# Issuing the stores of whole row tiles from ScalarE's DMA queue instead of SyncE's

## The chip, the core and the metric

The kernel runs on one core of a Trainium2 chip. A core has five engines, each with its own instruction stream: TensorE (PE in the profile, with PEld for its weight loads), VectorE (DVE), ScalarE (ACT), GpSimd (POOL) and SyncE (SP), which computes nothing and here only issues DMAs. An engine works through its stream strictly in order; where an instruction waits for a semaphore, all behind it wait too. DMAs are carried out by 16 DMA engines, and are issued by an instruction on SyncE or ScalarE, each of which has a queue of its own. The metric is the device time of one execution in microseconds, the median of several runs.

## What is computed

```python
batch, seq, dim = 8, 1024, 768          # x: float32 (8, 1024, 768)
# w_qkv: float32 (768, 2304)
rms = np.sqrt(np.mean(x ** 2, axis=-1, keepdims=True) + eps)
x_norm = x / rms * gamma
return np.matmul(x_norm, w_qkv)         # float32 (8, 1024, 2304)
```

So each of the 8192 rows of x is normalised, and the result is multiplied by one weight matrix.

## The kernel before

The rows are cut into 64 row tiles of 128 rows, and two neighbouring row tiles make a pair. The columns of the result are cut into three chunks of 768. One pair and one chunk make a 2 x 2 block problem (two row tiles, two halves of 384 columns, two halves of the 768 summed elements), and the kernel computes it with seven block products instead of eight: sums of blocks of x and sums of blocks of the weights are multiplied, and the results are put together from the products and held intermediate results. Such a product is three matmuls of 128x384.

The work on one pair passes through these steps:

- `load_x` (L417): SyncE issues the load of a row tile, 384 KB, into one of ten buffers.
- `pstat` and `prms` (L616, L620): ScalarE sums the squares and takes the root, `precip` (L625): VectorE takes the reciprocal.
- `pcast` (L630): VectorE scales the tile and casts it to float16, two instructions for a pair.
- `pxbar` (L634): SyncE issues a DMA transpose of the tile, so that the summed elements lie on the partitions.
- `osum` (L648): GpSimd makes four sums of blocks from the two transposed tiles, once both have landed, in one of three buffers.
- `product` (L668): TensorE, seven for each of the three chunks, into PSUM banks called a, b and c. A later product is added into the same bank after an earlier one has been copied out.
- `hold` (L677 on ScalarE, L675 on VectorE) copies an intermediate result out of PSUM; `join` (L684, VectorE) and `last` (L688, ScalarE) write finished blocks of 128x384 into the row tile's output buffer.
- `rstore` (L520): one DMA stores a whole row tile of 128x2304 float32, 1152 KB. In the very last pair `pstore` (L712) and `end_out` (L707) store pieces instead.

The order of instructions on each engine is written out by hand. The plan is a list of (time, operation) entries that is sorted by time and then issued; its times only order the instructions and make nothing happen at a moment. The first 15 pairs are listed in `PLAN`. From the 16th pair (`STEADY = 15`) on, a loop gives each chunk seven slots of 0.4875 us and each pair 21 slots, so 10.24 us, with the operations at fixed slots. A tile framework then adds the semaphores that the data need. It also gives each DMA one of eight DMA semaphores in turn, and a DMA is not issued before the one that had the same semaphore, eight DMAs earlier, has landed.

In the loop, a pair's first row tile is stored at slot 8.0 and its second at slot 15.6 of the last chunk, in the stream of SyncE, between the loads and the transposes of later pairs. In SyncE's stream the sequence of one pair is: store, store, load, load, transpose, transpose.

Of the kernel before, what the change touches and what calls it, by code (L numbers as in the profile page):

```python
# [350 lines left out]
def kernel(  # L351
# [8 lines left out]
    nc = tc.nc  # L360
# [10 lines left out]
    of = out.flatten_outer_dims()  # L371
# [3 lines left out]
    P = 128  # L375
# [37 lines left out]
    X, XB, XT, RS, OUT, WF, PM, PT = {}, {}, {}, {}, {}, {}, {}, {}  # L413
# [102 lines left out]
        else:  # L516
            nc.scalar.activation(out=o, in_=pm, func=AF.Copy, scale=RS[t], bias=0.0)

    def rstore(t):
        nc.sync.dma_start(out=of[t * P:(t + 1) * P, :], in_=OUT[t])  # L520
        if t in lent:
            spare.append(lent.pop(t))

# [2 lines left out]
    def at(time, fn, *args):  # L526
        plan.append((time, len(plan), fn, args))
# [181 lines left out]
    def pstore(p, c, i, *half):  # L709
# [4 lines left out]
    N_CH = N // (2 * CW)  # L714
    ops = {"load_x": load_x, "load_w": load_w, "conv": conv, "cast": cast, "stat": stat, "recip": recip, "tr": tr, "cp": cp, "mm": mm,
           "idle": idle, "gamma_in": gamma_in, "evac": evac, "rstore": rstore, "tr_half": tr_half, "cp_half": cp_half,
           "bound": bound, "fold": fold, "bound_tr": bound_tr, "bound_top": bound_top, "bound_all": bound_all,
           "scales": scales, "quad": quad, "tsum": tsum, "pstat": pstat, "prms": prms, "precip": precip, "pcast": pcast,
# [4 lines left out]
    for p in range(STEADY, MT // 2):  # L723
        for c in range(N_CH):
            z = HEAD_END + 7 * SLOT * ((p - STEADY) * N_CH + c)

            def when(u, fn, *args):
                at(z + u * SLOT, fn, *args)

            if c == 0:  # L730
                for i in range(2):
                    t = 2 * p + i
                    when(-96.3 + 0.1 * i, load_x, t)
                    when(-64 + 7 * i, pstat, t)
                    when(-48.1 + 1.3 * i, pcast, t)
                    when(-33.1 + 0.1 * i, pxbar, t)
                when(-54.5, prms, p)
                when(-48.3, precip, p)
                for i, q in enumerate(SUMS):
                    when(-15 + 0.01 * i, osum, p, q, "POOL")  # L740
            final = p == MT // 2 - 1
            end = final and c == N_CH - 1
            for i, u in ((1, 0), (5, 1), (2, 7.5 if end else 2), (6, 4), (3, 5), (7, 7 if end else 10), (4, 13)):
                if not (end and i == 4):
                    when(u, product, p, c, i)
            when(1.1, hold, p, c, "a", "p1", "ACT")
            when(2.1, hold, p, c, "c", "p5", "DVE" if c < 2 else "ACT")
            when(5.1, hold, p, c, "a", "u2", "ACT")
            if not end:
                when(5.3, join, p, c, 0, 0, "b", "p1")  # L750
                when(6.5, join, p, c, 0, 1, "c", "u2")
                if final:
                    when(8.0, pstore, p, c, 0)
                elif c == N_CH - 1:
                    when(8.0, rstore, 2 * p)
                when(11.1, join, p, c, 1, 1, "a", "p5")
                when(14.1, last, p, c)
                if final:
                    when(15.6, pstore, p, c, 1)
                elif c == N_CH - 1:  # L760
                    when(15.6, rstore, 2 * p + 1)
            else:
                when(6.5, join, p, c, 0, 1, "c", "u2")
                when(8.0, pstore, p, c, 0, 1)
                when(8.1, join, p, c, 1, 1, "a", "p5")
                when(9.0, pstore, p, c, 1, 1)
                when(9.1, join, p, c, 0, 0, "b", "p1")
                when(9.6, pstore, p, c, 0, 0)
                when(8.5, end_piece, p, c, 0)
                when(8.6, end_piece, p, c, 1)  # L770
                when(9.7, end_out, p, c, 0)
                when(9.8, end_out, p, c, 1)
# [39 lines left out]
```

## Time and profile before

| What | Before |
|---|---|
| Median of 3 runs | 353.65 us (353.23 to 354.0) |
| Span of the profiled execution | 351.6 us |
| Matmuls of the products (L668) | 1887, 326 ns each |
| Row tile stores (L520), issue to landing | 62, 7.2 to 7.3 us |
| Loads of x (L417), issue to landing | 64, 7.9 us |
| Transposes (L634), issue to landing | 56, 6.9 us |
| Bytes moved by the DMA engines | 119.17 MB, 339 GB/s on average |

The busy time of an engine is the sum of its instructions; issuing a DMA isn't counted in it. A row of the table of groups names the line, the engine, the operation and its tiles, the number of instructions, their busy time and the mean of one, and what ended the idle time before them. The chain that ended last follows the execution back from its end, always to what released the step. The median from issue to landing of a DMA counts the time in its queue as well.

### The profile page before, as it was taken

Reading aid. Unit: us, or ns where it says so; the run is one execution under the profiler, and the core shown is the slowest. Engines: PE = TensorE matmul, PEld = TensorE weight load, DVE = VectorE, ACT = ScalarE, POOL = GpSimd, SP = SyncE. Lnnn points to the kernel's source line nnn. Section 1 sums busy time; section 2 is a strip of 40 time slices with the busy share of each in tenths; the row PEclk is TensorE's granted clock in tenths of the full one; section 3 lists DMA queues with packets and bytes.
Section 4 is the critical chain, followed back from the end, with each engine's and each line's share of the span. In section 5 each row is a group of like instructions: output and inputs, shape, how many; then the busy total and the mean of one; then the engine's idle time right before and its main releaser. Section 6 shows DMA issues by size and latency. Waiting matters only on the chain.

```text
span 351.6 us, 6210 instructions
## 1 busy us (share of the span) xinstructions
PE 340.4 (97%) x2071; PEld 201.5 (57%) x2074; DVE 276.4 (79%) x506; ACT 240.9 (69%) x492; POOL 122.5 (35%) x134
## 2 busy tenths in 40 slices
PE   4999999999999999999999999999999999999995
PEld 2446556655666666666666565555655656666663
DVE  4789998989898897787677877788787778776663
ACT  5799998887654674866776767666766676664543
POOL 1386453261131254044404432434444143443400
PEclk9999999999999999999999999999999999999999
DMA  7999999989999999999999999999999999999757
GB/s 261 392 380 393 345 306 304 368 214 349 340 330 396 327 358 340 423 408 337 383 306 422 350 333 326 387 321 402 341 325 370 262 402 287 325 322 305 279 233 307
DMA packets 68381, 119.17 MB, mean 339 GB/s; under 512 B 47222, under 2 KB 48636, under 8 KB 60412
## 3 DMA queue, kind: packets, MB, share of 16 engines
q1 hardware_dynamic: 68192, 118.67, 101.9%
q8 instruction: 16, 0.26, 0.3%
q14 instruction: 17, 0.14, 0.1%
q10 hardware_dynamic: 156, 0.10, 0.1%
HBM read 32.25 MB, written 75.50 MB: 306 GB/s over the span
## 4 chain that ended last, share of the span: by engine, by line
PE 90%; DVE 4%; issue 2%; ACT 2%; DMA 1%; SPq 0%; DVEq 0%
PE pm L668 81%; PE pm L496 7%; DVE xb L630 2%; DMA x_t<-in_x_dram 1%; ACT pp L677 1%; DVE ot L684 1%; PE pm L537 1%; ACT wq L598 1%; PE pm L460 1%; PE pm L653 0%; DVE su L648 0%; DVE w_b L684 0%; PE pm L695 0%; DVE rstd L625 0%; ACT ot L688 0%
## 5 line engine op out<-in xcount | busy, mean ns | idle before, releaser
L668 PE MATMUL pm<-wq,su 128*128 128x384 f16 x1080 | 204.5, 326 | 0.4 <-ACT pp L677 0.4
L677 ACT ACTIVATE pp<-pm,sc 128x384 f32<-128x384 f32 x203 | 113.8, 580 | 80.5 <-PE pm L668 75.8
L668 PE MATMUL pm<-wq,xT 128*128 128x384 f16 x807 | 159.7, 326 | 1.8 <-DVE w_b L684 1.0
L668 PEld LDWEIGHTS <-su 128*128 128x128 f16 x1080 | 105.4, 98 | 70.1 <-issue 0.6
L684 DVE SCALAR_TENSOR_TENSOR ot<-pm,sc,pp 128x384 f32<-128x384 f32 x165 | 96.6, 612 | 22.8 <-PE pm L668 20.0
L668 PEld LDWEIGHTS <-xT 128*128 128x128 f16 x807 | 78.9, 98 | 55.4 <-issue 3.2
L648 POOL TENSOR_TENSOR su<-xT 128x384 f16<-128x384 f16 x54 | 51.1, 949 | 166.8 <-PE pm L668 104.7
L684 DVE SCALAR_TENSOR_TENSOR w_b<-pm,sc,pp 128x384 f32<-128x384 f32 x105 | 62.8, 611 | 9.7 <-PE pm L668 8.4
L675 DVE TENSOR_SCALAR pp<-pm,sc 128x384 f32<-128x384 f32 x67 | 40.8, 614 | 29.4 <-PE pm L668 29.1
L616 ACT ACTIVATE sq<-x_t 128x768 bf16<-128x768 f32 x60 | 50.2, 836 | 1.0 <-DMA x_t<-in_x_dram 0.8
L688 ACT ACTIVATE ot<-pm,sc 128x384 f32<-128x384 f32 x68 | 38.8, 577 | 12.7 <-PE pm L668 12.6
L630 DVE TENSOR_SCALAR xb<-x_t,rstd 128x768 f16<-128x768 f32 x60 | 45.4, 786 | 0.7
L648 POOL TENSOR_TENSOR su<-xT,su 128x384 f16<-128x384 f16 x26 | 26.0, 1001 | 10.9 <-DVE su L648 9.3
L648 POOL TENSOR_TENSOR su<-su,xT 128x384 f16<-128x384 f16 x24 | 23.4, 975 | 9.5 <-DVE su L648 7.8
L496 PE MATMUL pm<-w_b,xT 128*128 128x512 bf16 (+1 forms) x117 | 25.4, 364 | 0.1
L496 PEld LDWEIGHTS <-xT 128*128 128x128 bf16 x120 | 11.5, 100 | 10.8 <-issue 0.6
L688 ACT ACTIVATE w_b<-pm,sc 128x384 f32<-128x384 f32 x21 | 12.0, 578 | 5.2 <-PE pm L668 5.2
L432 POOL TENSOR_SCALAR w_b<-wq,g_sb 128x512 bf16<-128x512 f32 (+1 forms) x14 | 10.1, 729 | 15.4 <-DMA wq<-in_w_qkv_dram 15.4
L616 ACT ACTIVATION_READ_ACCUMULATOR sq<-x_t 128x1 f32 x60 | 11.5, 192 | 0.0
L600 POOL TENSOR_SCALAR wq<-w_b,inv 128x1152 f16<-128x1152 bf16 x8 | 9.7, 1228 | 1.6 <-DVE inv L584 1.6
L620 ACT ACTIVATE rms<-ssq,eps_sb 128x2 f32<-128x2 f32 x30 | 8.7, 293 | 0.2
L606 DVE TENSOR_TENSOR wq<-wq 128x1152 f16<-128x1152 f16 x11 | 8.6, 787 | 0.0
(53 smaller groups left out, 91.7 us busy)
## 6 DMA issues: line engine op xcount, KB each, us to landing
out_dram<-ot SPq DMA_DIRECT2D x42, 1152.0 KB, 7.3
x_t<-in_x_dram SPq DMA_DIRECT2D x64, 384.0 KB, 7.9
out_dram<-w_b SPq DMA_DIRECT2D x20, 1152.0 KB, 7.2
wq<-in_w_qkv_dram SPq DMA_DIRECT2D x10, 512.0 KB, 9.4
wq<-in_w_qkv_dram SPq DMA_DIRECT2D x4, 256.0 KB, 6.0
xT<-xb SPq DMA_TRANSPOSE x56, 6.9
wq<-in_w_qkv_dram SPq DMA_DIRECT2D x2, 384.0 KB, 9.7
out_dram<-w_b SPq DMA_DIRECT2D x2, 384.0 KB, 2.8
```

The lines of the kernel that those rows point to most:

```text
L432: nc.gpsimd.tensor_scalar(out=o, in0=i, scalar1=g, scalar2=1.0, op0=mult, op1=mult)
L496: nc.tensor.matmul(out=PM[t, n0][:, :nl], lhsT=XT[t][:, ko, :], rhs=w_b[:, ko, n0:n0 + nl], start=(b == 1), stop=(b == KO))
L600: nc.gpsimd.tensor_scalar(out=o, in0=quad_view(c, q), scalar1=INV[c], scalar2=1.0, op0=mult, op1=mult)
L616: nc.scalar.activation(out=sq, in_=X[t], func=AF.Square, accum_out=SS[p][:, t % 2:t % 2 + 1])
L620: nc.scalar.activation(out=r, in_=SS[p], func=AF.Sqrt, scale=inv_k, bias=eps_sb)
L630: nc.vector.tensor_scalar(out=XB[t], in0=X[t], scalar1=SS[t // 2][:, t % 2:t % 2 + 1], scalar2=None, op0=mult)
L648: (nc.vector if eng == "DVE" else nc.gpsimd).tensor_tensor(out=block(p, q), in0=block(p, x), in1=block(p, y), op=op)
L668: nc.tensor.matmul(out=PB[k][:, :CW], lhsT=block(p, a)[:, ko, :], rhs=WQ[c, b][:, ko, :], start=(first and ko == 0), stop=(ko == KO // 2 - ...
L675: nc.vector.tensor_scalar(out=o, in0=pb, scalar1=SC[c], scalar2=None, op0=mult)
L677: nc.scalar.activation(out=o, in_=pb, func=AF.Copy, scale=SC[c], bias=0.0)
L684: nc.vector.scalar_tensor_tensor(out=result(p, c, i, j), in0=PB[p, c, bank][:, :CW], scalar=SC[c], in1=PART[p, c, held], op0=mult, op1=add)
L688: nc.scalar.activation(out=result(p, c, 1, 0), in_=PB[p, c, "a"][:, :CW], func=AF.Copy, scale=SC[c], bias=0.0)
```

## The change

From the 16th pair on, the stores of whole row tiles are issued by ScalarE, over its own DMA queue. They stand somewhat later in the plan, at slots 9.5 and 17.0 instead of 8.0 and 15.6, so that the blocks of the row tile are finished when ScalarE comes to them. Loads and transposes stay on SyncE, and so do the stores of the first 15 pairs and most pieces of the last pair. The aim is that a store which waits for its data no longer holds up the loads and transposes behind it in SyncE's stream.

```diff
-    def rstore(t):
-        nc.sync.dma_start(out=of[t * P:(t + 1) * P, :], in_=OUT[t])
+    def rstore(t, eng="SP"):
+        (nc.scalar if eng == "ACT" else nc.sync).dma_start(out=of[t * P:(t + 1) * P, :], in_=OUT[t])
         if t in lent:
             spare.append(lent.pop(t))
...
                 elif c == N_CH - 1:
-                    when(8.0, rstore, 2 * p)
+                    when(9.5, rstore, 2 * p, "ACT")
...
                 elif c == N_CH - 1:
-                    when(15.6, rstore, 2 * p + 1)
+                    when(17.0, rstore, 2 * p + 1, "ACT")
```

In the streams of the built program, 32 stores leave SyncE and stand in ScalarE's: the first of a pair between two holds of the next pair's first chunk, the second just after `prms` in its second chunk. SyncE's sequence for a pair becomes load, load, transpose, transpose. All other engines' streams are the same.

## The prediction

> **What bounds the kernel now.** I read the page's busy table first, then windows over the part the change touches (from about 180 us, where the 16th pair is stored), then TensorE's waits there, then the chain.
>
> ```profile
> span 351.6 us, 6210 instructions
> ...
> PE 340.4 (97%) x2071; PEld 201.5 (57%) x2074; DVE 276.4 (79%) x506; ACT 240.9 (69%) x492; POOL 122.5 (35%) x134
> ```
> ```profile
> 180.00:220.00 40.00, 40.00 (x248) 24.05 (x246) 31.05 (x56) 27.88 (x60) 13.13 (x14) 1.00 1.09 350
> 220.00:265.00 45.00, 44.12 (x270) 26.14 (x268) 35.80 (x61) 30.30 (x66) 18.20 (x19) 1.00 1.07 356
> 265.00:300.00 35.00, 35.00 (x217) 21.06 (x216) 26.69 (x47) 23.94 (x53) 11.44 (x12) 1.00 1.10 319
> 300.00:345.00 45.00, 45.00 (x279) 27.07 (x278) 31.12 (x55) 25.69 (x52) 15.00 (x16) 1.00 0.85 304
> ```
> Columns: stretch, its length, busy us (count) of PE, PEld, DVE, ACT, POOL, granted clock, DMA share, GB/s. PE is busy 164.12 of 165 us: **all that any change here can give back is 0.88 us** (0.25%), since the tail after 346 us is small stores that the change leaves alone. The DMA share of about 1.1 until 300 us says that the DMA engines are full as well: hidden, but with little to spare.
>
> ```profile
> PE pm L668 <- DVE ot L684: 0.5, 2, 0.3
> PE pm L668 <- DVE w_b L684: 0.3, 1, 0.3
> ```
> ```profile
> 218.80 0.17 DVE rstd L625
> ...
> 219.99 1.27 DVE xb L630
> 221.26 0.54 DVE ot L684
> 221.79 0.04 issue
> 221.84 6.51 PE pm L668 x39
> ```
> TensorE's only waits are on joins (L684) which came late because the two casts (L630) ahead of them were slow. VectorE's timeline has these two at 2.27 us together at 218.99, where GpSimd adds the operand sums (L648) at the same time, and 1.18 us at 188.23, where it has just finished. When GpSimd adds is set by the landing of the second transpose (its waits name DMA xT), so the DMA queue does reach TensorE, weakly.
>
> Next, ScalarE's slack around the place of the first store of a pair, in its timeline:
>
> ```profile
> 192.07 0.58 ACT L677 ACTIVATE pp<-pm,sc 128x384 f32<-128x384 f32 x1
> 193.72 0.58 ACT L677 ACTIVATE pp<-pm,sc 128x384 f32<-128x384 f32 x1 [1.06 <-PE pm L668]
> 194.20 0.83 ACT L616 ACTIVATE sq<-x_t 128x768 bf16<-128x768 f32 x1
> 194.93 0.19 ACT L616 ACTIVATION_READ_ACCUMULATOR sq<-x_t 128x1 f32 x1
> 195.02 0.57 ACT L688 ACTIVATE w_b<-pm,sc 128x384 f32<-128x384 f32 x1
> 195.49 0.58 ACT L677 ACTIVATE pp<-pm,sc 128x384 f32<-128x384 f32 x1
> ```
> The store goes in at 192.65, into an idle 1.06 us. After it ScalarE works without a gap up to the hold that ends at 196.07; TensorE's next product into that bank is the second of three in a block that begins at 195.95 (1.63 us for three), so at about 196.5. Slack after the gap: some 0.4 us.
>
> Last, SyncE's timeline, the order and times of the transfers:
>
> ```profile
> 180.32 0.54 SPq L520 DMA_DIRECT2D out_dram<-ot  x1
> 181.33 0.34 SPq L520 DMA_DIRECT2D out_dram<-w_b  x1
> 185.38 0.33 SPq L520 DMA_DIRECT2D out_dram<-ot  x1
> 185.76 0.95 SPq L417 DMA_DIRECT2D x_t<-in_x_dram  x2
> 186.81 6.27 SPq L634 DMA_TRANSPOSE xT<-xb  x2
> 193.19 0.52 SPq L520 DMA_DIRECT2D out_dram<-ot  x1
> ```
> **What the Trainium skill says.** "DMA: Bandwidth & Descriptors", Issuing engines are not separate DMA queues: issuing from several engines saves only the issue time, as all run on the same 16 DMA engines; its section Queues, rings and completion order adds that each DMA engine takes packets in turn from the queues that have work. Before has one busy queue, so no trace here shows the sharing. "Perfetto Trace Analysis", DMA Instruction — HWDGE: the sequencer holds the shared descriptor generator while it issues, and another one waits for the lock. Not visible before either, but a transpose holds SyncE for 1.21 to 4.03 us (median 1.94, by its line), a store 0.33 to 0.35 when nothing is ahead. "SBUF — State Buffer", Who interferes with whom: a VectorE tensor_scalar in a two-port mode and a GpSimd operation exclude each other. The trace agrees: a cast takes 0.60 us alone, up to 1.28 beside GpSimd.
>
> **The change part by part.** Removed: 32 store issues of 0.34 us on SyncE, worth nothing there by themselves, as SyncE computes nothing. Added: the same 32 on ScalarE, at the 0.38 us of the one store that it issues already (L707): 32 x 0.38 = 12.2 us on an engine 65% busy here. Hidden: the first store of a pair lies in the 1.06 us gap, the second behind the statistics' L620 in the 0.88 us gap before 197.13.
>
> Moved: SyncE's order. Before, a store held up the loads and transposes behind it. Casts of 177.99 us were transposed only at 186.81. With the stores gone a transpose can start when its cast ends, so SyncE runs most of a pair (10.24 us) ahead: in the stretch just after 181 us two loads and a transpose, and soon two more loads, enter a DMA queue that is full already.
>
> A new wait. In the built program the DMAs take eight semaphores in turn, and each waits for the landing of the one eight earlier. For a store on ScalarE that is now a load or transpose that SyncE issued, and all of ScalarE's evacuations stand behind it; TensorE waits for those. ScalarE can lose 1.06 - 0.38 + 0.4 = 1.05 us without TensorE noticing. A pair's second store waits for a transpose or load issued as long before but has 4 us more: I take no wait there.
>
> Costs of transfers, as estimates from bytes over the 350 GB/s of the first stretch: store 1.18 MB, 3.4 us; load 0.39 MB, 1.1 us; for a transpose what is left of a pair's 10.24 us, (10.24 - 6.8 - 2.2) / 2 = 0.6 us (upper end: its median issue, 1.94).
>
> The 17th pair's first store is ready at 192.65 and waits for the first early transpose. Before, the store of 181.33 landed after 8.8 us, at 190.2, so the queue is full until then. Behind it now: two loads, the transpose, and, if turns are taken, the next store, which comes on the other queue at about 186.3. 190.2 + 2.2 + 0.6 = 193.0 without that store, + 3.4 = 196.4 with it: a wait of 0.4 to 3.7 us, so a TensorE stall of 0 to 2.7. The 18th pair's first store waits for a load with 5.1 us of loads and transposes and two stores ahead of it: 196.4 + 5.1 + 6.8 = 208.3, against its ready time of 202.9 + 2.7 = 205.6. Wait 2.7, stall 1.6. The 19th: 218.5 against 217.4, wait 1.1, stall about 0: the stalls have given the DMA engines time to work off what was issued early. Sum 0 to 4.3 us; I take **3.5**, near the upper end, as the overtaking store comes 2 us before the queue is free.
>
> A gain. Transposes started at the cast land, once the queue is worked off, some 5.5 us after it instead of about 17, so GpSimd's 3.9 us are over at about the time of the next casts, and the slow pairs of casts go: 0 to 0.88 us. In the pairs where the queue is still long they can still meet: I take 0.5. The final stores cost nothing: the same engines issue them, and the last ones land in 1.9 to 2.4 us.
>
> Sum: 353.65 + 3.5 - 0.5 = 356.65, say **356.6 us**.
>
> **The rivals.** (a) The waits stay within the 1.05 us, because the other queue's store does not overtake or two queues move more than one; then only the gain is left: 353.65 - 0.8 = 352.8 us. For it: the wait's lower end, 0.4, is under the slack, and after 220 us stores land in 6.1 us (median) against 7.8 before, so the queue is not always full. Against: the early stretch is where SyncE jumps ahead. (b) Nothing moves: the waits are hidden and GpSimd meets the casts as often as now, or a small stall eats the gain: 353.6. For it: PE is 100% busy in three of the four stretches. (c) ScalarE's stores wait for the descriptor generator while SyncE's transposes hold it. A transpose holds up to 3.4 us before 225 us; over the slack that is 2.3 us, and in three or four pairs 7 to 9: about 361 us. Against: casts end, and so transposes start, nearly 4 us ahead of the first store of a pair, and two of them take 3.3 us when the queue is not full.
>
> **How the numbers follow.** Forecast 0.47, (a) 0.28, (b) 0.15, (c) 0.10. Slower: forecast and (c), 0.57. Same: (b), and the part of (a) that wins under 0.7 us: 0.18. Faster: the rest of (a), 0.25. The range goes from (a) with all its gain, 352.7, to the forecast with its full stall of 4.3 and a little more from 0.6 us transposes being too short, 358.8; (c) and slivers at both ends stay out.
>
> **What would show it.** Right: in the profile after, PE idle of 1 to 3 us around 196 and 206 us, released by ScalarE (pp L677); ScalarE's queue with semaphore waits of 2 to 4 us just ahead of L520 there and none late; transposes starting within 1 us of their casts; the casts near 0.6 us in the last ten pairs; everything up to 181 us as now. Wrong: no semaphore wait over 1 us ahead of ScalarE's L520 (then rival a or b); L520 itself lasting 1 to 3 us on ScalarE (then c); or PE waits spread evenly over all pairs, which neither a start-up queue nor the casts explain.

## The result and the profile after

| | Before | After |
|---|---|---|
| Median on the same chip | 353.44 us (352.85 to 354.0) | 364.49 us (362.68 to 394.29) |
| Ratio | | 1.0296, 95% interval 1.0241 to 1.0351 |
| Span of the profiled execution | 351.6 us | 361.7 us |
| Mean granted TensorE clock | 1.0 | 0.984 |

The change costs 11 us by the medians, against 3 predicted. The ratio leaves out one slow execution of 394.29 us, and by it the cost is 10.5 us. The direction was right, the size was not. The stretches again, now after the change, with the same columns as in the prediction:

```profile
180.00:220.00 40.00, 33.64 (x178) 18.64 (x177) 23.14 (x41) 20.37 (x44) 14.43 (x16) 0.88 1.12 318
220.00:265.00 45.00, 45.00 (x277) 27.07 (x276) 32.27 (x61) 30.89 (x67) 14.45 (x16) 1.00 1.08 340
265.00:300.00 35.00, 35.00 (x217) 21.03 (x215) 26.26 (x47) 23.88 (x52) 10.86 (x12) 1.00 1.03 344
300.00:345.00 45.00, 44.75 (x277) 26.83 (x275) 32.02 (x57) 27.27 (x54) 14.95 (x16) 1.00 0.74 261
```

All of the loss lies in one stretch of 40 us. There TensorE is busy for 33.64 us instead of 40.00, and it runs at a mean clock of 0.88 instead of 1.00: two losses, not one. From 220 us on TensorE is as full as before, though 26 of the 32 moved stores are issued there.

What TensorE waited for from 170 us on, and what ScalarE waited for between 180 and 225 us (waiter, releaser: us in total, times, longest):

```profile
PE pm L668 <- ACT pp L677: 6.4, 4, 2.4
PE pm L668 <- DVE ot L684: 0.3, 1, 0.3
```
```profile
ACT pp L677 <- DMA x_t<-in_x_dram: 5.2, 1, 5.2
ACT pp L677 <- DMA xT<-xb: 5.1, 1, 5.1
```

TensorE idles for 6.4 us for holds. They were late because a store ahead of them in ScalarE's stream waited: once for a transpose, once for a load. A store needs neither of them for its data. They are the DMAs eight places earlier in the built program, which had the same semaphore. The first of the two places, in the timeline of all engines:

```profile
191.84 0.58 ACT L677 ACTIVATE pp<-pm,sc 128x384 f32<-128x384 f32 x1
...
197.13 0.34 ACTq L520 DMA_DIRECT2D out_dram<-ot  x1
197.51 0.58 ACT L677 ACTIVATE pp<-pm,sc 128x384 f32<-128x384 f32 x1 [5.10 <-DMA xT<-xb]
...
198.15 0.65 PE L668 MATMUL pm<-wq,su 128*128 128x384 f16 x3 [2.24 <-ACT pp L677]
...
199.91 2.08 PE L668 MATMUL pm<-wq,su 128*128 128x384 f16 x6 [1.12 <-ACT pp L677]
```

ScalarE is free at 192.42 and issues the store at 197.13: 4.71 us of waiting, for a transpose issued at 183.94 that landed after 13.12 us, at 197.06. TensorE starts again at 198.15, waits once more while ScalarE catches up, and then takes 2.08 us for six matmuls that take 1.14 at full clock. Stretches around the two places, cut where the granted clock changes and into pieces of equal length (the columns as above), show why:

```profile
196.45:199.86 3.41, 0.65 (x3) 0.29 (x3) 1.67 (x3) 2.35 (x6) 1.77 (x2) 1.00 1.15 352
199.86:203.27 3.41, 3.36 (x11) 1.62 (x11) 1.75 (x4) 1.05 (x4) 1.83 (x3) 0.50 1.13 388
203.27:206.68 3.41, 3.41 (x23) 2.05 (x21) 1.95 (x5) 2.40 (x5) 0.00 (x0) 1.00 1.53 32
210.10:213.51 3.41, 1.36 (x9) 0.69 (x7) 0.00 (x0) 0.32 (x1) 1.95 (x3) 1.00 1.13 277
213.51:216.92 3.41, 2.45 (x8) 1.07 (x8) 2.35 (x4) 2.38 (x7) 1.54 (x2) 0.50 1.18 393
216.92:220.34 3.42, 3.42 (x13) 1.57 (x11) 2.20 (x4) 1.57 (x3) 2.07 (x3) 0.50 0.96 404
```

Shortly after each stall the granted clock is 0.50, for 3.4 us after the first and 6.8 us after the second, while TensorE is mostly at work again. Half of the busy time in the three pieces at 0.50 is 1.7 + 1.2 + 1.7 = 4.6 us, which is what the slow clock costs.

To place gains and losses I compare the start times of ScalarE's 203 holds (L677) with those of before, one by one; below this is called the lag, and its times are those of the kernel before. It is -0.2 us up to 192 us, +5.1 at 201, +11.2 at 213, falls to +9.7 at 272 and ends at +10.1. So the two stalls with their slow clock cost 5.3 and 6.1 us, and the pairs after them give 1.5 back, 0.4 of which is lost again.

### The profile page after: what moved, and what is told of

Read it like the earlier page. It is cut to its first block, busy times and chain, and to the rows that moved or that the text cites. A ratio compares the mean times of both kernels' runs of the same rounds, so it can differ in the third digit from the quotient of the medians.

```text
span 361.7 us, 6189 instructions
## 1 busy us (share of the span) xinstructions
PE 344.3 (95%) x2074; PEld 202.5 (56%) x2074; DVE 272.4 (75%) x506; ACT 241.1 (67%) x492; POOL 119.5 (33%) x134
## 4 chain that ended last, share of the span: by engine, by line
PE 83%; DMA 8%; ACT 2%; DVE 2%; SPq 2%; issue 1%; ACTq 0%; DVEq 0%
PE pm L668 76%; PE pm L496 6%; DMA x_t<-in_x_dram 4%; DMA out_dram<-ot 2%; DMA wq<-in_w_qkv_dram 2%; ACT pp L677 1%; DVE xb L630 1%; SPq L634 1%; ACT wq L598 1%; SPq L417 1%; DVE ot L684 0%; PE pm L653 0%; SPq L422 0%; DVE su L648 0%; ACT w_b L430 0%
## 5 line engine op out<-in xcount | busy, mean ns | idle before, releaser
L668 PE MATMUL pm<-wq,su 128*128 128x384 f16 x1080 | 207.6, 329 | 6.9 <-ACT pp L677 6.9
L677 ACT ACTIVATE pp<-pm,sc 128x384 f32<-128x384 f32 x203 | 113.9, 580 | 88.5 <-PE pm L668 74.2
L668 PE MATMUL pm<-wq,xT 128*128 128x384 f16 x807 | 161.5, 329 | 1.2 <-DVE w_b L684 0.8
L648 POOL TENSOR_TENSOR su<-xT 128x384 f16<-128x384 f16 x54 | 50.2, 932 | 172.5 <-DMA xT<-xb 98.9
L630 DVE TENSOR_SCALAR xb<-x_t,rstd 128x768 f16<-128x768 f32 x60 | 41.1, 713 | 0.7
L648 POOL TENSOR_TENSOR su<-xT,su 128x384 f16<-128x384 f16 x26 | 25.1, 967 | 10.9 <-DVE su L648 9.2
L648 POOL TENSOR_TENSOR su<-su,xT 128x384 f16<-128x384 f16 x24 | 22.1, 921 | 9.5 <-DVE su L648 7.8
L496 PEld LDWEIGHTS <-xT 128*128 128x128 bf16 x120 | 11.3, 98 | 11.2 <-issue 0.6
L432 POOL TENSOR_SCALAR w_b<-wq,g_sb 128x512 bf16<-128x512 f32 (+1 forms) x14 | 10.1, 730 | 15.2 <-DMA wq<-in_w_qkv_dram 14.5
```

The lines of the kernel that those rows point to most:

```text
L432: nc.gpsimd.tensor_scalar(out=o, in0=i, scalar1=g, scalar2=1.0, op0=mult, op1=mult)
L496: nc.tensor.matmul(out=PM[t, n0][:, :nl], lhsT=XT[t][:, ko, :], rhs=w_b[:, ko, n0:n0 + nl], start=(b == 1), stop=(b == KO))
L630: nc.vector.tensor_scalar(out=XB[t], in0=X[t], scalar1=SS[t // 2][:, t % 2:t % 2 + 1], scalar2=None, op0=mult)
L648: (nc.vector if eng == "DVE" else nc.gpsimd).tensor_tensor(out=block(p, q), in0=block(p, x), in1=block(p, y), op=op)
L668: nc.tensor.matmul(out=PB[k][:, :CW], lhsT=block(p, a)[:, ko, :], rhs=WQ[c, b][:, ko, :], start=(first and ko == 0), stop=(ko == KO // 2 - ...
L677: nc.scalar.activation(out=o, in_=pb, func=AF.Copy, scale=SC[c], bias=0.0)
```

## The experiments

**Theory:** where the stores change over to ScalarE, SyncE is no longer held up and issues loads and transposes ahead into full DMA engines. ScalarE's stores then wait for the landing of such a DMA eight earlier, TensorE stalls, and its clock halves afterwards. The rest of the change is nearly free. **Rivals:** a price for each store issued on ScalarE (32 x 0.34 us is 10.9 us, just the loss); the later slots; the second queue itself, whose stores overtake SyncE's transfers; and, for the slow clock, a cause other than the stall. The descriptor generator, the prediction's last rival, was settled by the changed kernel itself: no store on ScalarE took longer than 0.38 us to issue between 181 and 225 us.

### The late slots without ScalarE

```diff
-                    when(9.5, rstore, 2 * p, "ACT")
+                    when(9.5, rstore, 2 * p)
-                    when(17.0, rstore, 2 * p + 1, "ACT")
+                    when(17.0, rstore, 2 * p + 1)
```

> All stores stay on SyncE, but at the late slots 9.5 and 17.0. Theory (the loss is ScalarE's wait for the landing of the DMA eight earlier, in the two pairs after the hand-over, and the slow TensorE clock behind each stall): no store stands in ScalarE's stream, so no stall; 353 to 355 us. Rival 'late slots' (stores, and with them the loads and transposes behind them, simply come later): a good part of the 11 us, 357 us or more. Rival 'price per issue' (32 issues of 0.34 us on ScalarE add up to 10.9 us): 353.5 us.

352.08 us, ratio 0.9942 (0.9918 to 0.9965): 0.6% faster than before, so the late slots cost nothing. They are a small gain by themselves. From 180 to 345 us TensorE waits for nothing.

### ScalarE with the old slots

```diff
-                    when(9.5, rstore, 2 * p, "ACT")
+                    when(8.0, rstore, 2 * p, "ACT")
-                    when(17.0, rstore, 2 * p + 1, "ACT")
+                    when(15.6, rstore, 2 * p + 1, "ACT")
```

> The 32 stores on ScalarE, but at the old slots 8.0 and 15.6. Theory: the semaphore turns differ a little (the 17th pair's first store now waits for the landing of the 16th pair's second store, the 18th's for a transpose), but both are young DMAs in a full queue; TensorE stalls by 1.5 to 3 us once or twice and its clock drops: 357 to 366 us. Rival 'late slots': back to 353.5 us. Rival 'price per issue': 364 us with TensorE's idle time spread over all pairs.

360.82 us, ratio 1.0174 (1.0119 to 1.0229). In the built program the 17th pair's first store now has its semaphore from the 16th pair's second store, and that is what ScalarE waits for (timeline of ScalarE):

```profile
191.68 0.57 ACT L688 ACTIVATE w_b<-pm,sc 128x384 f32<-128x384 f32 x1
196.56 0.34 ACTq L520 DMA_DIRECT2D out_dram<-ot  x1
197.00 0.58 ACT L677 ACTIVATE pp<-pm,sc 128x384 f32<-128x384 f32 x1 [4.75 <-DMA out_dram<-ot]
```

TensorE's gap is 4.35 us, the lag goes from +0.1 to +6.3, and no second stall of this kind follows. Another DMA eight earlier, the same stall: the turn of the semaphores decides what is waited for, not the kind of transfer.

### The change from the 23rd pair on

```diff
-                    when(9.5, rstore, 2 * p, "ACT")
+                    when(9.5 if p >= 22 else 8.0, rstore, 2 * p, "ACT" if p >= 22 else "SP")
-                    when(17.0, rstore, 2 * p + 1, "ACT")
+                    when(17.0 if p >= 22 else 15.6, rstore, 2 * p + 1, "ACT" if p >= 22 else "SP")
```

> Stores go to ScalarE only from the 23rd pair on (p >= 22, 18 stores); before that all as in the kernel before. Theory: the hand-over now lies at about 253 us; the second pair's first store waits there for a transpose six places earlier in SyncE's stream, and the queue is full there as well: a stall of 1 to 3 us near 264 us and a slow clock after it, 356 to 362 us, and nothing at 196 or 212 us. Rival 'backlog of the head' (only the queue left by the first 15 pairs is long enough): no stall over 0.5 us, 353 to 354 us. Rival 'price per issue': 18 x 0.34 = 6.1 us, spread over nine pairs, 359.6 us.

360.35 us, ratio 1.0168 (1.0115 to 1.0220). TensorE has gaps of 2.64 us at 279.6 and 1.12 at 282.8, with a lag of 6.9 us from that place alone, and nothing of the kind at 196 or 212. The hand-over brings its stall along, a pair later than I expected. (For the 2.64 us the view of waits names GpSimd's sum L648, which ended at 282.15, next to ScalarE's hold, which ended at 282.14. It was the hold: the sums just then being made are those which the kernel before begins only at 280.14, after it has begun the same product at 279.42.) SyncE's waits between 262 and 285 us, one issue from its timeline, and the chain of waits from 268 to 285 us (start, us, what):

```profile
SPq L634 <- DMA out_dram<-w_b: 8.8, 1, 8.8
```
```profile
269.04 6.08 SPq L634 DMA_TRANSPOSE xT<-xb  x1
```
```profile
274.69 0.43 SPq L634
275.12 0.04 issue
275.16 5.93 DMA x_t<-in_x_dram
...
281.17 0.34 ACTq L520
281.51 0.05 issue
281.56 0.59 ACT pp L677
```

Here the load that ScalarE's store waited for was not slow (5.93 us). It was issued late. SyncE's transposes had stood 8.8 us, up to 262.70, for a store that ScalarE had issued at 253.88 to land, and of the four transposes that followed, the last held SyncE for 6.08 us, up to 275.12, for a reason that the trace does not show. Two in-order queues that share one ring of semaphores can wait for each other in turn, and ScalarE passes its wait on to TensorE.

### Two of the 32 stores back on SyncE

```diff
-                    when(9.5, rstore, 2 * p, "ACT")
+                    when(8.0 if p in (16, 17) else 9.5, rstore, 2 * p, "SP" if p in (16, 17) else "ACT")
```

> The changed kernel with just two of its 32 stores, the first ones of the 17th and 18th pair, back on SyncE at slot 8.0: those on which ScalarE waited 4.7 us. If only the backlog at 181 us makes the waits, these stalls go and nothing replaces them: 352 to 354.5 us. If the hand-over itself makes them (SyncE, no longer held up, issues ahead, and the next store of ScalarE waits for something that it issued late), the stall moves to the next pairs, between 215 and 240 us: 356 to 362 us.

356.93 us, ratio 1.0073 (1.0051 to 1.0095). The two old stalls are gone, and a new one stands at 218.5 us (2.09 and then 1.12 us of gap). TensorE's waits from 175 us on, and ScalarE's between 212 and 225 us:

```profile
PE pm L668 <- ACT pp L677: 3.5, 3, 2.1
```
```profile
ACT pp L677 <- DMA xT<-xb: 5.1, 1, 5.1
```

The stall moved with the place where SyncE comes free, as in the run from the 23rd pair. The profiled execution took 360.7 us, more than all others of this kernel but one, so it shows the place of the stall and not its usual size.

### The change from the 28th pair on, without loads

The same edit as for the 23rd pair, with 27 in place of 22.

> Stores go to ScalarE only from the 28th pair on (p >= 27, 8 stores), when the loads are over and the DMA engines are 85% busy. Theory: the hand-over costs time only where the DMA engines are full and SyncE has loads and transposes to issue ahead; here the DMA eight earlier has landed when ScalarE comes to its store: no stall over 0.5 us, 353 to 354.5 us. Rival 'price per issue': 8 x 0.34 = 2.7 us, 356.4 us. Rival 'any hand-over stalls': 356 to 361 us, with a TensorE gap over 2 us near 305 to 325 us.

354.51 us, ratio 1.0008 (0.9991 to 1.0025). ScalarE waits for no DMA, TensorE's longest gap is 0.52 us, behind a join, and the clock stays at 1.00. The eight stores issued on ScalarE cost nothing that can be measured. Neither a price per issue (356.4) nor a stall at any hand-over whatever holds. This place lacks two things, full DMA engines and loads that SyncE can issue ahead; which of them a stall needs, the run does not tell.

### Only the first, and only the second store on ScalarE

```diff
-                    when(17.0, rstore, 2 * p + 1, "ACT")
+                    when(15.6, rstore, 2 * p + 1)
```

> Only the first store of each pair on ScalarE (slot 9.5), the second on SyncE at slot 15.6, ahead of the loads and transposes. Theory: ScalarE's stores wait for transposes of the pair before, issued 6 to 9 us earlier; with landings of 7 to 10 us this leaves waits around 0 to 3 us, and the slack hides 1: 353 to 357 us. Rival 'price per issue': 359 us.

The runs lie between 356.2 and 370.4 us, so the ratio, 1.0096 (1.0053 to 1.0139), rests on the two lowest of five. ScalarE waits for no DMA in the profiled run (358.7 us). TensorE has two gaps, 1.05 and 1.25 us near 203 and 205 us, as a transpose landed only 15.7 us after it was issued at 188.09 and the sums came late; the clock is then 0.50 from 205.32 to 208.73 us. TensorE's waits from 175 us on:

```profile
PE pm L668 <- POOL su L648: 1.2, 1, 1.2
PE pm L668 <- DMA xT<-xb: 1.0, 1, 1.0
```

This loss is not the theory's, as no store on ScalarE waited. It is what the rival of the second queue says.

```diff
-                    when(9.5, rstore, 2 * p, "ACT")
+                    when(8.0, rstore, 2 * p)
```

> Only the second store of each pair goes to ScalarE (slot 17.0); the first stays on SyncE at slot 8.0. Theory: SyncE is still held up once a pair, and in the built program ScalarE's stores now wait for stores issued a pair or so earlier, which have mostly landed: no TensorE stall over 0.5 us and no slow clock, 352.8 to 354.5 us. Rival 'price per issue': 16 x 0.34 = 5.4 us, 359 us. Rival 'two queues' (a store on a second queue overtakes and delays SyncE's transfers, whatever ScalarE waits for): 356 us or more, with TensorE waiting for sums.

355.01 us, ratio 1.0026 (1.0002 to 1.0050). ScalarE waits for no DMA. TensorE's waits from 175 us on:

```profile
PE pm L668 <- DVE ot L684: 0.4, 1, 0.4
PE pm L695 <- DVE ot L684: 0.2, 1, 0.2
```

No stall; in the built program its stores have their semaphores from older DMAs. The 16 issues do not cost 5.4 us. The median is half a microsecond above the expected range, and the profile, of a run of 354.29 us, doesn't show where that is.

### The slow clock by itself

```diff
+            if c == 0 and p in (18, 22, 26):
+                for i in range({18: 5, 22: 8, 26: 12}[p]):
+                    when(1.05 + 0.001 * i, pause)
```

Here `pause` is a 128x512 copy of a constant into a scratch tile on ScalarE, added to the kernel before.

> The kernel before, with extra work on ScalarE that nothing needs (128x512 copies of a constant, estimated 0.5 us each) just ahead of the first hold of three pairs: 5 of them in the 19th (about 202 us), 8 in the 23rd (about 245 us), 12 in the 27th (about 288 us). Less ScalarE's slack of some 1.5 us, TensorE should stall 1, 2.5 and 4.5 us. Theory (TensorE's clock drops after a stall of about 2 us or more, whatever caused it): clock 1.00 after the first, 0.5 for some 3 us after the second and third, so the time grows by the stalls, 8 us, and 2 to 3 us for each drop: about 366 us. Rival (the slow clock of the changed kernel comes from something else than the stall): clock 1.00 throughout, 361.5 us.

372.74 us, ratio 1.0534 (1.0511 to 1.0556); the gaps came out longer than I had estimated: 2.35, 4.33 and 7.02 us, with small ones of 0.5 to 0.6 in between. Windows around the first (stretch, length, TensorE busy, clock, DMA share, GB/s):

```profile
196.00:204.00 8.00, 7.49 (x47) 1.00 0.95 366
204.00:207.00 3.00, 0.65 (x5) 1.00 1.18 266
207.00:210.00 3.00, 3.00 (x12) 0.55 1.09 429
210.00:213.00 3.00, 3.00 (x18) 0.88 0.97 332
213.00:240.00 27.00, 27.00 (x168) 1.00 1.10 312
```

and around the second:

```profile
250.00:255.00 5.00, 0.67 (x6) 1.00 0.72 272
255.00:258.00 3.00, 3.00 (x11) 0.52 0.00 0
258.00:261.00 3.00, 3.00 (x18) 0.91 0.95 332
```

With all stores on SyncE a plain stall gives the same picture: half clock for 3.4 us (0.55 or 0.52 and then 0.88 or 0.91, as means over pieces of 3 us), and the drop comes late, here when TensorE is already working again. For the first stall that is 3 x 0.45 + 3 x 0.12 = 1.7 us on top of 2.35 of idling; the lag grew by 4.8, 6.7 and 9.9 us at the three places, small gaps included. A stall is enough for the slow clock, whatever made it; nothing else is needed to explain it in the changed kernel.

It is not the length of a gap that counts, though. The traces record the granted clock, and in all of them it changes only in steps of 3.41 us. Cut a trace into windows on that grid, which lies differently in each run, and TensorE's busy time in one window tells the clock of the next. In the fourteen traces together there are 1407 complete windows at full clock. After 47 of them the clock is 0.50, and none of these has over 1.51 us of work; after the other 1360 it stays at 1.00, and none of these has under 1.46 us. At half clock it stays low after up to 2.72 us of work and comes back after 2.77 us or more. So the two short gaps with only the first stores on ScalarE were enough, as they left 1.51 us of work in one window, while a gap of 2.95 us at 291.25 in the run with 16 rows (below) cost no clock, as it fell across two windows:

```profile
201.91:205.32 3.41, 1.51 (x9) 0.51 (x6) 1.18 (x3) 2.36 (x5) 0.57 (x1) 1.00 1.08 390
205.32:208.73 3.41, 3.02 (x10) 1.46 (x11) 0.62 (x1) 0.00 (x0) 3.02 (x4) 0.50 1.05 431
```
```profile
289.41:292.82 3.41, 1.84 (x12) 0.88 (x9) 1.65 (x3) 2.35 (x5) 0.00 (x0) 1.00 1.09 213
292.82:296.23 3.41, 2.03 (x13) 1.14 (x14) 0.97 (x2) 0.00 (x0) 2.84 (x4) 1.00 0.96 398
```

### Holding SyncE up with a small part of each store

```diff
-        (nc.scalar if eng == "ACT" else nc.sync).dma_start(out=of[t * P:(t + 1) * P, :], in_=OUT[t])
+        r = {"SP": (0, P), "row": (0, 1), "ACT": (1, P)}[eng]
+        (nc.scalar if eng == "ACT" else nc.sync).dma_start(out=of[t * P + r[0]:t * P + r[1], :], in_=OUT[t][r[0]:r[1], :])
...
+                    when(8.0, rstore, 2 * p, "row")
...
+                    when(15.6, rstore, 2 * p + 1, "row")
```

> As the changed kernel, but SyncE stores one row (9 KB) of each row tile at the old slots 8.0 and 15.6, and ScalarE the other 127 rows at 9.5 and 17.0. SyncE is held up for the data as in the kernel before, and there are eight DMAs per pair, so that ScalarE's store waits for its own predecessor, one pair back, or for something as old. Theory: no wait over 1 us ahead of ScalarE's stores, no stall, no slow clock: 352.5 to 355 us with all 32 large stores still on ScalarE. Rival 'price per issue': 364 us. Rival 'two queues' (stores on a queue of their own delay the transposes, whatever ScalarE waits for): 357 us or more, with TensorE or GpSimd waiting for transposes.

1644.96 us, ratio 4.6465 (4.6377 to 4.6552): it says nothing on the theory. A store of 127 rows held ScalarE at its issue for up to 45 us (timeline of ScalarE):

```profile
255.29 45.10 ACTq L521 DMA_DIRECT2D out_dram<-w_b  x1
300.44 0.58 ACT L678 ACTIVATE pp<-pm,sc 128x384 f32<-128x384 f32 x1 [44.52 <-issue]
```

The Trainium skill has the reason, which the edit had overlooked: "DMA: Bandwidth & Descriptors", Why a DMA increments its semaphore by 16 and not by 1, says that the number of DMA engines must divide the size of the slowest dimension, and that 127 partitions put everything on one. The trace agrees: some 27 GB/s while these stores run, against about 350 before. So again with 16 and 112 rows (the edit has 16 in place of 1):

> The run with one row on SyncE again, with 16 rows (147 KB) of each row tile stored by SyncE at slots 8.0 and 15.6 and 112 rows by ScalarE at 9.5 and 17.0, because 127 rows moved at some 27 GB/s. SyncE is held up for the data as in the kernel before; there are eight DMAs per pair, so ScalarE's store waits for its own predecessor or something as old. Theory: no wait over 1 us ahead of ScalarE's stores, no stall, no slow clock: 352.5 to 355 us. Rival 'price per issue': 364 us. Rival 'two queues': 357 us or more, with TensorE waiting for sums or transposes.

407.91 us, ratio 1.1395 (1.1305 to 1.1485). One half of the theory's expectation came true: from 175 us on ScalarE waits for DMAs for 0.8 us in all. The other half did not:

```profile
PE pm L669 <- POOL su L649: 23.3, 7, 7.8
PE pm L669 <- DMA xT<-xb: 11.5, 2, 6.6
```

TensorE now waits for sums and transposes. SyncE is held up for the data as before, and its transposes then land late (one issued at 193.10 after 14.65 us). So stores on a second queue can hurt the transposes without any wait on ScalarE, as the rival of two queues has it; in the changed kernel itself TensorE waits for no transpose, but ScalarE's first wait is for one, and how much of its 13.12 us is owed to the second queue no run tells. But here the pieces also move worse: 263 GB/s at a DMA share of 1.12 between 220 and 265 us, where the kernel before has 356 at 1.07. How much is the queue and how much the pieces stays open, and so does a kernel with 32 whole stores on ScalarE, none of which waits.

### Where the gain of the late slots is

```diff
-                    when(15.6, rstore, 2 * p + 1)
+                    when(17.0, rstore, 2 * p + 1)
```

> No store on ScalarE; only the second store of each pair moves, from slot 15.6 to 17.0 on SyncE, which puts it behind the two loads and two transposes instead of ahead of them. If the gain of the run with both late slots comes from transposes that start about 4 us earlier (and adds that no longer meet the casts), this gives it all: 351.5 to 352.5 us, transposes issued some 3 to 4 us earlier than before in the pairs after 190 us, casts near 0.62 us. If it comes from the first store's later slot: 353.5 us.

351.72 us, ratio 0.9938 (0.9920 to 0.9956), as with both slots. The store of slot 15.6 stood just ahead of a pair's loads and transposes on SyncE; at 17.0 it stands behind them. GpSimd's first sums of a pair, in its timelines, before and in this run:

```profile
207.86 0.91 POOL L648 TENSOR_TENSOR su<-xT 128x384 f16<-128x384 f16 x1 [5.94 <-PE pm L668]
208.86 1.26 POOL L648 TENSOR_TENSOR su<-su,xT 128x384 f16<-128x384 f16 x1
```
```profile
203.35 0.91 POOL L648 TENSOR_TENSOR su<-xT 128x384 f16<-128x384 f16 x1 [5.82 <-PE pm L668]
204.34 0.91 POOL L648 TENSOR_TENSOR su<-su,xT 128x384 f16<-128x384 f16 x1
```

The two casts of this pair start at 208.73 before and take 1.81 us beside the sums; here they start at 208.14, when the sums are over, and take 1.15. (The brackets name TensorE, but the sums start here just after the second transpose has landed, at 203.2.) Over all pairs from 181 us on, by the casts' line (minimum, median, maximum in ns):

```profile
L630 DVE TENSOR_SCALAR xb<-x_t,rstd x26: 607/872/1276, 188.2 to 313.2; 128x768 f16<-128x768 f32 x26
```
```profile
L630 DVE TENSOR_SCALAR xb<-x_t,rstd x26: 612/620/1262, 187.7 to 311.2; 128x768 f16<-128x768 f32 x26
```

The lag goes from -0.6 at 201 us to -2.1 at 272, in steps at the places where casts and sums no longer meet. That is 1.5 us; the first 0.6 are there before any moved store and are a difference between two executions. Both stores behind the transposes, at slots 16.9 and 17.0 on SyncE, should have kept this gain:

> No store on ScalarE; on SyncE both stores of a pair move behind the loads and transposes (slots 16.9 and 17.0), so that no load or transpose stands behind a store of its own pair's data. This is the aim of the change without the second queue. If the transposes' start is all that there is to gain, 351.5 to 352.5 us, as with the second store alone, since TensorE has no idle time left there; if a store 4 us later holds up the output buffers, TensorE waits for joins and it is slower than 354 us.

355.11 us, ratio 1.0019 (1.0007 to 1.0032): a miss. The lag falls to -1.2 at 250 us, but then both casts of a pair meet the sums (sums from 248.59 us beside casts from 249.63, which take 2.46), TensorE waits 0.52 us at 252.16, and the lag ends at -0.3. Not the earliest transposes are best here, but sums that fall between two pairs' casts.

## Why the prediction was wrong in size

**What bounds the kernel** was right, with one number too low. The most that could be gained was put at 0.88 us from TensorE's busy time. The late second store alone moves the lag by 1.4 us between 201 and 320 us, so the busy shares taken from the trace hid half a microsecond. ScalarE's slack adds up to 1.08 us rather than 1.05, which changes nothing.

**The issues** were right: 0.34 to 0.38 us each, hidden. **SyncE running ahead** was right: from 203 us on transposes start within 1 us of their casts, loads right behind.

**The wait of the 17th pair's first store** was right in kind and place, short in size. The transpose was to land at 193.0 to 196.4; it landed at 197.06. That is 0.7 us beyond the upper end, and TensorE's gaps are 2.24 + 1.12 = 3.4 us where at most 2.7 were allowed for. The transpose was issued 2.9 us earlier than in the kernel before (183.94 against 186.81) and landed 0.4 us later (197.06 against 196.70): in full DMA engines an earlier issue bought nothing.

**The wait of the 18th pair's first store** is the queue term that was mis-sized. Predicted: landing at 208.3, wait 2.7, stall 1.6. Measured: the load was issued at 198.30, between two stores of ScalarE's queue at 197.13 and 199.42, and landed after 14.42 us, at 212.72. ScalarE waited 4.8 us (208.00 to 212.80), and TensorE's gaps are 2.36 + 0.65 = 3.0 us. It stands at 211.5 instead of 206 us, as the first stall delays it by 5.3. The transfers that landed between the two, from 197.06 to 212.9 us, are the ones that had been counted: three loads, three transposes, two stores. Their price was too low, 11.9 us where 15.7 passed. Some 3.4 us of that lie in one piece shown above, 203.27 to 206.68 us, in which the DMA engines are occupied (share 1.53) but move 32 GB/s, where 350 had been assumed. The kernel before has shorter dips of this kind (114 GB/s from 194 to 196 us); why this one is so long stays open. **The 19th pair's** stall was put at about 0, and there is none.

**The step that failed outright is the one that isn't there**: that a stalled TensorE costs its idle time and no more. The prediction converted waits into stalls and stalls into time one to one, and a granted clock of 1.00 in all of its stretches was no warning, since the kernel before has no stall there. The slow clock after the stalls cost 4.6 us. "TensorE: Matmul & The Clock Gate", Part 1 of the Trainium skill, states that the clock is half after at least one idle window of about 3.4 us, and that the window runs freely. The runs here agree on the half clock and on windows of 3.41 us, and differ on how idle a window has to be: some 1.5 us of work in it did not keep the clock up, so a gap of 2.35 us was enough (the first of the stall run), and so were gaps of 1.05 and 1.25 us shortly after each other (first store alone on ScalarE); the measurement decides.

**The gain** of 0.5 us was right in kind: the median cast after the change takes 0.62 us, and the lag falls by 1.5 us after the stalls. Four pairs still meet the sums.

The sum anew: 6.4 us of stalls instead of 3.5, 4.6 us of slow clock instead of nothing, 1.1 us of net gain instead of 0.5, so 9.9 against 10.1 by the spans. **The rivals:** (a) and (b), waits within the slack, are refuted by the 4.7 and 4.8 us. (c), the descriptor generator, gave nearly the right time for a reason that the trace refutes.

The aim, a store that no longer holds up loads and transposes, was met without the second queue: the second store behind the transposes on SyncE, 0.9938. It beats both kernels.

## What to carry to other kernels

Before a DMA moves to an engine that computes, ask not what its issue costs but what its issue may have to wait for: with completion semaphores in turn, that is the landing of somebody else's DMA, and all of the engine's work stands behind it. Count 1.7 to 3 us on top of a TensorE stall of 2 us or more, since the clock can be slow for one or two windows of 3.41 us afterwards; a shorter stall can cost this too when another is near, and one that falls across two windows can escape it. And when a store holds up loads in one queue, first try its place in that queue.

## What was not expected of the hardware

- The granted clock changes in steps of 3.41 us: it drops to 0.50 after a window with less than about 1.5 us of TensorE work and comes back after one with 2.77 us or more. So it drops 2 to 5 us after a stall begins, mostly when TensorE is busy again. A gap of 2.35 us cost 1.7 us more that way, and one of 2.95 us nothing.
- A store of 127 rows moves at some 27 GB/s and can hold the issuing engine for 45 us; with 128 rows it is issued in 0.34 us.
- A load issued in the midst of two queues' stores took 14.42 us to land, where the kernel before needs 9.1 us between 180 and 220 us (median).
